# Two activation sums of the up projection: from GpSimd to VectorE, and later in the order

## The chip, the core and the metric

The kernel runs on one core of one Trainium2 chip. A core has TensorE (PE in the profile) for matrix products, VectorE (DVE), ScalarE (ACT), GpSimd (POOL) and SyncE (SP). SP and POOL also issue transfers here: SP's go through queue q1 of the profile, POOL's through q0. The metric is the device time of one execution in microseconds. The time before is the median of three runs; a profiled execution has a time of its own, and a span (first to last instruction) a little shorter than that.

## The reference, cut to what matters

One layer of an encoder on 512 rows of width 1024: a mixing part (a recurrent group and an attention group), then a feed-forward part, which the change lies in.

```python
x = x + concat(RMSNorm(rnn_out), RMSNorm(attn_out)) @ W_out
x = x + relu(RMSNorm(x) @ W_up)^2 @ W_down      # W_up 1024 x 4096, W_down 4096 x 1024
```

All of it is float32.

## The kernel before

**Products.** A float32 product is made of three reduced-precision ones (`mm3`, lines 319 to 322): both operands are split into a high part (ScalarE copies to fp32r: `whi`, `hh`) and a remainder (VectorE subtracts: `wlo`, `hl`), and high x high, high x low, low x high are summed in PSUM.

**Fewer products.** The up and down projections use a scheme with seven products of 2 x 2 blocks in place of eight. It needs sums of weight blocks and sums of activation blocks. The weight sums are mostly made by transfers that POOL issues and that add to what lies in SBUF (`accum_op=OP.add`); the activation sums are made by the engines in `h_sum` (line 1328). With `a = hm[k]` and `b = hm[k+4]` (the normalised, transposed activations), each 128 x 512, `left` and `right` the halves of the sequence, there are four sums:

- t1 = b.right - a.right, by VectorE
- t2 = -a.left - t1, by VectorE
- t3 = a.left - a.right, by GpSimd
- 22 = a.left - b.left + t1, by GpSimd in two instructions

Each sum has four quarters (k = 0 to 3) of 128 x 256; two quarters make one tile `hsum`. After every second quarter SP stores the tile to DRAM (`hsd`, line 1343, 256 KB), from where the second half of the projection loads it again. Two tiles make a sum, and `split_h` splits each of them (ScalarE `hh` line 1359, VectorE `hl` line 1362).

**Steps.** The up projection runs in two halves (`half` 0 and 1) of 28 steps each. A step is named by block column and product, for example 8:21, and has 24 products of 128 x 256 (lines 1547 to 1553). The first half goes 0:11, 8:11, 4:11, 0:21, 8:21, 4:21, 0:t1, 8:t1, 0:t2, 0:22, 0:t3, 8:t2, 8:22, 4:t1, 0:t4, 8:t3, 4:t2, 8:t4 and on. While step s computes, the weights of step s + 3 are split (`feed`, line 307: `whi` at product pair 2, `wlo` at pair 4). The dictionary `late` hangs further work on a step and a pair n.

**Order.** PE, ACT, DVE and POOL execute in the order in which the program is written. SP's order is made by a planner before the ninth step and is the written one from there on. What is late on an in-order engine delays all behind it.

**Buffers.** A plain weight block goes into one of three `wraw` buffers; `emit_dma` (line 225) loads the next one when `wlo` of an earlier block is made (line 270). Blocks that need sums lie in one of four `tw` buffers: `load_t` (line 1187) loads them on SP, `add_t` (line 1194) and `conv_lo` (lines 278 and 286) add further blocks through POOL, and line 282 adds a block with VectorE. The tiles of 128 x 512 share 45 slots.

**Around the beginning.** The product with W_out ends with the steps "s1" and "22" of `OSEQ`. VectorE adds its results into `x1n` (line 1218), PE transposes these (`h2_t`, line 1221), ScalarE writes `h2h` (line 1229) and `hm` (line 1231), and VectorE the remainder `h2l` (line 1234). The second half of the transposes stands inside steps 0:11 and 8:11.

Of the kernel before, what the change touches and what calls it, by code (L numbers as in the profile page):

```python
# [15 lines left out]
OP = mybir.AluOpType  # L16
# [85 lines left out]
def hybrid_kernel(ctx: ExitStack, tc, xw0, xw, xn, w_in, w_v, w_out, w_up, w_dn, gates, vecs, bias, fg, out):  # L102
    nc = tc.nc
# [9 lines left out]
    stt = nc.vector.scalar_tensor_tensor  # L113
    NG = 45

    def g_(name, dt=FT, shape=(P, S)):
        return work.tile(list(shape), dt, name=name, tag="g", bufs=NG)
# [633 lines left out]
    for n, (k, tt) in enumerate(steps):  # L751
        c = C_V + k // 2
# [434 lines left out]
    def load_t(half, n, f0, adds=True):  # L1187
        t = work.tile([P, 1024], FT, name="tw", tag="tw", bufs=4)
        nc.sync.dma_start(t, ublock(half, "12", f0))
        raws[cq[half, f0, n]] = t  # L1190
        if adds:
            add_t(half, n, f0)

    def add_t(half, n, f0):
        for b in {"t1": ("11",), "t2": ("11", "22"), "t3": ("22",) if (half, f0) in ADDED else ()}[n]:
            nc.gpsimd.dma_start(raws[cq[half, f0, n]], ublock(half, b, f0), accum_op=OP.add)
# [24 lines left out]
    def h2_t(k, tag):  # L1221
        if not hb:
            hb["h"] = big.tile([P, KD, S], FR, name="h2h", tag="bigB")
            hb["l"] = [t[:, j, :] for c in ("bigC", "bigD") for t in (big.tile([P, KD // 2, S], FR, name="h2l", tag=c),) for j in range(KD // 2)]
        pt = ps_("pxt", tag)
        n, j = k // 4, k % 4
        for tt in range(4):
            nc.tensor.transpose(pt[:, tt * P:(tt + 1) * P], x1n[tt, n][:, j * P:(j + 1) * P], ident)
        act(hb["h"][:, k, :], pt, AF.Copy, scale=vec("mg", k))
        hm[k] = g_("hm")  # L1230
        act(hm[k], pt, AF.Copy, scale=vec("mg", k))

    def h2_l(k):
        nc.vector.tensor_tensor(hb["l"][k], hm[k], f(hb["h"])[:, k, :], op=OP.subtract)
# [29 lines left out]
    for w in OSEQ:  # L1264
        for i in range(4):
            tt, k = i // 2, i % 2
# [59 lines left out]
    left, right = slice(0, TH), slice(TH, S)  # L1326

    def h_sum(n, k):
        m, c = k // 2, slice((k % 2) * TH, (k % 2 + 1) * TH)
        if k % 2 == 0:  # L1330
            hsum[n, m] = hsr[n, m] = g_("hsum")
        a, b, o = hm[k], hm.get(k + 4), hsr[n, m][:, c]
        if n == "t1":
            nc.vector.tensor_tensor(o, b[:, right], a[:, right], op=OP.subtract)
        elif n == "t2":
            stt(o, a[:, left], -1.0, hsr["t1", m][:, c], op0=OP.mult, op1=OP.subtract)
        elif n == "t3":
            nc.gpsimd.tensor_tensor(o, a[:, left], a[:, right], op=OP.subtract)
        else:
            nc.gpsimd.tensor_tensor(o, a[:, left], b[:, left], op=OP.subtract)  # L1340
            nc.gpsimd.tensor_tensor(o, o, hsr["t1", m][:, c], op=OP.add)
        if k % 2:
            nc.sync.dma_start(hsd[SUMS.index(n)][:, m * S:(m + 1) * S], hsr[n, m])

    hsr = {}
# [11 lines left out]
    def h_hi(n, m):  # L1357
        hsp[n, m] = (g_("hh", FR), g_("hl", FR))
        act(hsp[n, m][0], hsum[n, m], AF.Copy)

    def h_lo(n, m):
        nc.vector.tensor_tensor(hsp[n, m][1], hsum.pop((n, m)), f(hsp[n, m][0]), op=OP.subtract)
# [139 lines left out]
    def add_s1(half, ts, q):  # L1502
        t = raws[cd_[half] + 2 * q + 1] = ts[:, q, :]
        nc.gpsimd.dma_start(t, wblock(half, "12", q), accum_op=OP.add)
# [9 lines left out]
    for half in range(2):  # L1514
# [58 lines left out]
        def split_h(n, m):  # L1573
            def run():
                h_hi(n, m)
                h_lo(n, m)
            return run

        def xt(tt, n):
            return lambda: x1_sq(tt, n)  # L1580
# [16 lines left out]
        if half == 0:  # L1597
            def more():
                t, r = raws[cq[0, 12, "t3"]], st.pop("r")
                nc.vector.tensor_tensor(t, t, r, op=OP.add)  # L1600

            def sums(*a):
                return lambda: [h_sum(n, k) for n, k in a]

            def turn(js):
                def run():
                    for j in js:
                        h2_t(j, "et" if j < 6 else "pj")
                        h2_l(j)
                return run  # L1610

            late.update({(0, "11", 0): lambda: conv_lo(C_WA + 8), (0, "11", 3): lambda: conv_lo(C_WA + 9), (0, "11", 6): turn((4, 5)), (8, "11", 1): turn((6, 7)),
                         (0, "11", 1): sums(*[("t3", k) for k in range(4)]), (8, "11", 0): sums(("t1", 0), ("t1", 1)), (8, "11", 5): split_h("t1", 0),
                         (4, "11", 0): sums(("t1", 2), ("t1", 3), ("22", 0), ("22", 1), ("22", 2), ("22", 3)),
                         (4, "11", 1): split_h("t1", 1), (0, "21", 0): sums(("t2", 0), ("t2", 1)),
                         (0, "21", 5): split_h("t2", 0), (8, "21", 0): sums(("t2", 2), ("t2", 3)), (8, "21", 5): split_h("t2", 1),
                         (4, "21", 5): split_h("22", 0), (0, "t1", 5): split_h("22", 1),
                         (0, "t3", 3): put, (8, "t2", 3): put, (8, "t1", 1): split_h("t3", 0), (0, "t2", 1): split_h("t3", 1),
                         (8, "21", 2): lambda: load_t(0, "t1", 4, False), (4, "21", 2): lambda: add_t(0, "t1", 4), (8, "11", 7): lambda: add_t(0, "t3", 0),
                         (8, "t1", 5): lambda: load_t(0, "t3", 8),  # L1620
                         (8, "t2", 6): lambda: load_t(0, "t3", 4), (0, "t4", 3): put, (8, "t3", 0): lambda: load_t(0, "t1", 12, False), (4, "t2", 2): lambda: add_t(0, "t1", 12),
                         (4, "t3", 0): lambda: load_t(0, "t3", 12, False), (12, "t1", 7): more,
                         (0, "22", 7): xt(0, 0), (8, "t2", 7): xt(0, 1), (0, "t4", 7): room,
                         (12, "11", 5): lambda: add_s1(half, ts, 0), (4, "t4", 1): lambda: add_s1(half, ts, 1), (12, "t2", 1): lambda: add_s1(half, ts, 2), (12, "22", 5): lambda: add_s1(half, ts, 3)})
        else:
            late.update({(0, "11", 1): split_h(*HSEQ[6]), (0, "t1", 1): split_h(*HSEQ[7])})
# [100 lines left out]
        if half == 1:  # L1727
            b = 6 * NQ
# [89 lines left out]
```

## Time and profile before

| | |
|---|---|
| time, median of 3 runs | 528.49 us (526.54 to 528.83) |
| time of the profiled execution | 526.84 us |
| its span | 525.1 us |
| PE busy | 515.9 us (98%) |
| DVE busy | 428.3 us (82%) |
| ACT busy | 361.4 us (69%) |
| POOL busy | 85.2 us (16%) |
| DMA, mean over the span | 208 GB/s |
| granted TensorE clock | 0.998 |

A row of a timeline reads: start in us, duration in us, engine, line, operation, output<-input, shape, count, and in brackets the idle time before it with what ended it. A row of waits reads: who waited for whom, us in total, times, the longest. A row of windows gives the window, its length, the busy time of each engine with its number of instructions in brackets, the granted clock, the busy share of the DMA engines and GB/s. A line on a queue gives packets, MB and share of the time of 16 DMA engines.

### The profile page before, as it was taken

Reading aid. Unit: us, or ns where it says so; the run is one execution under the profiler, and the core shown is the slowest. Engines: PE = TensorE matmul, PEld = TensorE weight load, DVE = VectorE, ACT = ScalarE, POOL = GpSimd, SP = SyncE. Lnnn points to the kernel's source line nnn. Section 1 sums busy time; section 2 is a strip of 40 time slices with the busy share of each in tenths; the row PEclk is TensorE's granted clock in tenths of the full one; section 3 lists DMA queues with packets and bytes.
Section 4 is the critical chain, followed back from the end, with each engine's and each line's share of the span. In section 5 each row is a group of like instructions: output and inputs, shape, how many; then the busy total and the mean of one; then the engine's idle time right before and its main releaser. Section 6 shows DMA issues by size and latency. Waiting matters only on the chain.

```text
span 525.1 us, 8396 instructions
## 1 busy us (share of the span) xinstructions
PE 515.9 (98%) x3093; PEld 445.7 (85%) x3093; DVE 428.3 (82%) x655; ACT 361.4 (69%) x581; POOL 85.2 (16%) x109
## 2 busy tenths in 40 slices
PE   9999999999999998999999999999999999999995
PEld 7857888778787788999999888888999999888884
DVE  6998995887877889778689986889665977987885
ACT  7579946668765847577868965566567677655664
POOL 0182000000000427420112131001101300131000
PEclk9999999999999999999999999999999999999999
DMA  8736545358796499698879999986987497699704
GB/s 287 227 94 196 162 144 180 111 161 223 189 291 214 91 192 254 231 250 217 240 160 309 272 267 273 303 301 161 281 266 175 110 226 209 161 299 259 180 2 160
DMA packets 41465, 109.34 MB, mean 208 GB/s; under 512 B 5168, under 2 KB 13488, under 8 KB 41424
## 3 DMA queue, kind: packets, MB, share of 16 engines
q1 hardware_dynamic: 32576, 78.63, 44.7%
q0 software_dynamic: 8704, 29.99, 30.6%
q8 instruction: 24, 0.39, 0.3%
q10 hardware_dynamic: 144, 0.20, 0.1%
q14 instruction: 17, 0.14, 0.1%
HBM read 99.78 MB, written 4.29 MB: 198 GB/s over the span
## 4 chain that ended last, share of the span: by engine, by line
PE 85%; DMA 5%; DVE 4%; issue 3%; ACT 1%; POOL 1%; DVEq 0%; POOLq 0%; ACTq 0%
PE pd L320 10%; PE pd L321 10%; PE pd L322 10%; PE pu L320 7%; PE pu L321 7%; PE pu L322 7%; DMA tw<-in_w_up_dram 4%; PE pqk L320 3%; PE pqk L322 3%; PE pqk L321 3%; PE pt L850 2%; PE ps L814 2%; PE pwo L320 2%; PE pwo L322 2%; PE pwo L321 2%
## 5 line engine op out<-in xcount | busy, mean ns | idle before, releaser
L270 DVE TENSOR_TENSOR wlo<-wraw,whi 128x1024 fp32r<-128x1024 f32 x70 | 86.3, 1236 | 27.3 <-ACT whi L248 27.2
L248 ACT ACTIVATE whi<-wraw 128x1024 fp32r<-128x1024 f32 x66 | 69.3, 1053 | 38.4 <-PE pd L322 15.3
L321 PE MATMUL pd<-wlo,ah 128*128 128x512 f32 (+1 forms) x195 | 75.2, 386 | 0.0
L320 PE MATMUL pd<-whi,ah 128*128 128x512 f32 (+1 forms) x195 | 75.2, 386 | 0.0
L322 PE MATMUL pd<-whi,al 128*128 128x512 f32 (+1 forms) x195 | 75.2, 386 | 0.0
L320 PE MATMUL pu<-hh,whi 128*128 128x256 f32 x256 | 72.4, 283 | 0.0
L321 PE MATMUL pu<-hl,whi 128*128 128x256 f32 x256 | 72.4, 283 | 0.0
L322 PE MATMUL pu<-hh,wlo 128*128 128x256 f32 x256 | 72.4, 283 | 0.0
L270 DVE TENSOR_TENSOR wlo<-tw,whi 128x1024 fp32r<-128x1024 f32 x41 | 50.0, 1220 | 18.6 <-ACT whi L248 18.6
L248 ACT ACTIVATE whi<-tw 128x1024 fp32r<-128x1024 f32 x42 | 44.3, 1056 | 25.2 <-DMA tw<-in_w_up_dram 12.0
L322 PE MATMUL pu<-h2h,wlo 128*128 128x256 f32 x184 | 52.2, 283 | 0.9 <-DVE wlo L270 0.9
L320 PE MATMUL pu<-h2h,whi 128*128 128x256 f32 x184 | 52.3, 284 | 0.1
L321 PE MATMUL pu<-h2l,whi 128*128 128x256 f32 x184 | 52.0, 283 | 0.0
L320 PEld LDWEIGHTS pu<-hh,whi 128*128 128x128 f32 x256 | 49.2, 192 | 0.0
L321 PEld LDWEIGHTS pu<-hl,whi 128*128 128x128 f32 x256 | 49.2, 192 | 0.0
L322 PEld LDWEIGHTS pu<-hh,wlo 128*128 128x128 f32 x256 | 49.2, 192 | 0.0
L322 PEld LDWEIGHTS pd<-whi,al 128*128 128x128 f32 x195 | 36.6, 188 | 7.4
L320 PEld LDWEIGHTS pd<-whi,ah 128*128 128x128 f32 x195 | 36.6, 188 | 7.3
L321 PEld LDWEIGHTS pd<-wlo,ah 128*128 128x128 f32 x195 | 36.6, 188 | 7.3
L248 ACT ACTIVATE whi<-ts 128x1024 fp32r<-128x1024 f32 x24 | 25.4, 1059 | 21.4 <-PE pd L322 14.7
L270 DVE TENSOR_TENSOR wlo<-ts,whi 128x1024 fp32r<-128x1024 f32 x24 | 29.3, 1222 | 8.9 <-ACT whi L248 8.6
L322 PEld LDWEIGHTS pu<-h2h,wlo 128*128 128x128 f32 x184 | 35.3, 192 | 1.1 <-DVE wlo L270 1.1
(282 smaller groups left out, 1251.4 us busy)
## 6 DMA issues: line engine op xcount, KB each, us to landing
wraw<-in_w_up_dram SPq DMA_DIRECT2D x24, 512.0 KB, 4.3
wraw<-in_w_dn_dram SPq DMA_DIRECT2D x24, 512.0 KB, 9.9
ts<-in_w_dn_dram POOLq DMA_DIRECT2D x24, 512.0 KB, 12.0
tw<-in_w_up_dram POOLq DMA_DIRECT2D x22, 512.0 KB, 7.9
tw<-in_w_up_dram SPq DMA_DIRECT2D x17, 512.0 KB, 6.1
wraw<-in_w_in_dram SPq DMA_DIRECT2D x13, 512.0 KB, 4.2
ts<-in_w_dn_dram SPq DMA_DIRECT2D x8, 512.0 KB, 6.5
tw<-in_w_dn_dram SPq DMA_DIRECT2D x8, 512.0 KB, 6.8
```

Source lines behind the costliest of these rows:

```text
L248: act(hi, raws[i], AF.Copy)
L270: nc.vector.tensor_tensor(lo, r, f(splits[i][0]), op=OP.subtract)
L320: nc.tensor.matmul(o, lhsT=a[0], rhs=b[0], start=bool(first), stop=False, skip_group_check=on)
L321: nc.tensor.matmul(o, lhsT=a[0], rhs=b[1], start=False, stop=False, skip_group_check=on)
L322: nc.tensor.matmul(o, lhsT=a[1], rhs=b[0], start=False, stop=bool(last), skip_group_check=on)
L814: nc.tensor.matmul(psq[p, u][e][:, :NK], lhsT=qs_[p, a][r, P * qt:P * qt + P], rhs=kks[p][r, b, w:w + NK], start=i == 0, stop=i == 2)
L850: nc.tensor.transpose(pt[:, i * P:(i + 1) * P], en[h][qt][:, k:k + P], ident)
```

## The change

VectorE makes t3 and 22. The sum 22 is one instruction for a quarter instead of two: -b.left - t2, which is the same as a.left - b.left + t1. Both stand later: t3 moves from step 0:11 to 8:t1, and 22 from 4:11 to 0:t1; the splits of 22 go from 4:21 and 0:t1 to 0:t1 and 8:t1, those of t3 from 8:t1 and 0:t2 to 0:t2 alone (pairs 1 and 5). The stores to `hsd` follow the sums. GpSimd only issues transfers in this part.

```diff
         elif n == "t3":
-            nc.gpsimd.tensor_tensor(o, a[:, left], a[:, right], op=OP.subtract)
+            nc.vector.tensor_tensor(o, a[:, left], a[:, right], op=OP.subtract)
         else:
-            nc.gpsimd.tensor_tensor(o, a[:, left], b[:, left], op=OP.subtract)
-            nc.gpsimd.tensor_tensor(o, o, hsr["t1", m][:, c], op=OP.add)
+            stt(o, b[:, left], -1.0, hsr["t2", m][:, c], op0=OP.mult, op1=OP.subtract)
...
-                         (0, "11", 1): sums(*[("t3", k) for k in range(4)]), (8, "11", 0): sums(("t1", 0), ("t1", 1)), (8, "11", 5): split_h("t1", 0),
-                         (4, "11", 0): sums(("t1", 2), ("t1", 3), ("22", 0), ("22", 1), ("22", 2), ("22", 3)),
+                         (8, "11", 0): sums(("t1", 0), ("t1", 1)), (8, "11", 5): split_h("t1", 0),
+                         (4, "11", 0): sums(("t1", 2), ("t1", 3)),
...
-                         (4, "21", 5): split_h("22", 0), (0, "t1", 5): split_h("22", 1),
-                         (0, "t3", 3): put, (8, "t2", 3): put, (8, "t1", 1): split_h("t3", 0), (0, "t2", 1): split_h("t3", 1),
+                         (0, "t1", 0): sums(*[("22", k) for k in range(4)]), (0, "t1", 5): split_h("22", 0), (8, "t1", 1): split_h("22", 1),
+                         (0, "t3", 3): put, (8, "t2", 3): put, (8, "t1", 3): sums(*[("t3", k) for k in range(4)]), (0, "t2", 1): split_h("t3", 0), (0, "t2", 5): split_h("t3", 1),
```

## The prediction

> **What bounds the kernel now.** The page first: its opening lines say that PE is busy for all but 2% of the span. So a change in another engine can only pay where PE waits, and the next view is the waits of PE over the whole span.
>
> ```profile
> span 525.1 us, 8396 instructions
> PE 515.9 (98%) x3093; PEld 445.7 (85%) x3093; DVE 428.3 (82%) x655; ACT 361.4 (69%) x581; POOL 85.2 (16%) x109
> ```
> ```profile
> PE pxt L1228 <- DVE x1n L1218: 1.4, 1, 1.4
> PE pu L322 <- DVE wlo L270: 0.9, 1, 0.9
> ```
>
> Two waits of any size, both for VectorE, and both by the sixth step of the up projection. PE's timeline has them exactly, with a small third one:
>
> ```profile
> 201.89 0.27 PE L1228 MATMUL pxt<-ident,x1n 128*128 128x128 f32 x1
> 203.61 0.99 PE L1228 MATMUL pxt<-ident,x1n 128*128 128x128 f32 x7 [1.44 <-DVE x1n L1218]
> ...
> 218.01 0.28 PE L320 MATMUL pu<-h2h,whi 128*128 128x256 f32 x1
> 218.13 0.28 PE L321 MATMUL pu<-h2l,whi 128*128 128x256 f32 x1
> 219.33 0.39 PE L322 MATMUL pu<-h2h,wlo 128*128 128x256 f32 x1 [0.92 <-DVE wlo L270]
> ...
> 222.07 0.28 PE L320 MATMUL pu<-hh,whi 128*128 128x256 f32 x1
> ...
> 253.63 0.28 PE L322 MATMUL pu<-hh,wlo 128*128 128x256 f32 x1
> 254.01 0.39 PE L320 MATMUL pu<-h2h,whi 128*128 128x256 f32 x1
> ```
>
> A product of this stage starts 0.12 us after the one before (218.01, 218.13), so a step of 24 takes 2.88. The gaps above that pace: 203.61 - 201.89 - 0.12 = 1.60, 219.33 - 218.13 - 0.12 = 1.08, and 254.01 - 253.63 - 0.12 = 0.26. Together 2.94 us, the most that this stage can give. Now VectorE and GpSimd before the first gap:
>
> ```profile
> 197.44 3.59 DVE L1234 TENSOR_TENSOR h2l<-hm,h2h 128x512 fp32r<-128x512 f32 x2
> ...
> 201.61 1.28 DVE L1234 TENSOR_TENSOR h2l<-hm,h2h 128x512 fp32r<-128x512 f32 x2
> 202.81 0.74 DVE L1218 SCALAR_TENSOR_TENSOR x1n<-pwo,nrc,x 128x512 f32<-128x512 f32 x1
> 203.47 3.48 DVE L270 TENSOR_TENSOR wlo<-wraw,whi 128x1024 fp32r<-128x1024 f32 x3
> ```
> ```profile
> 198.03 3.60 POOL L1338 TENSOR_TENSOR hsum<-hm 128x256 f32<-128x256 f32 x4
> ```
>
> The same pair of `h2l` takes 3.59 us where GpSimd makes t3 beside it and 1.28 where it doesn't: 2.31 lost. The last `x1n`, which PE waits for, is late by it. Before the second gap the pattern repeats with sum 22:
>
> ```profile
> 212.71 1.75 DVE L270 TENSOR_TENSOR wlo<-wraw,whi 128x1024 fp32r<-128x1024 f32 x1 [2.13 <-ACT whi L248]
> 214.39 0.68 DVE L1362 TENSOR_TENSOR hl<-hsum,hh 128x512 fp32r<-128x512 f32 x1
> 216.44 1.16 DVE L1362 TENSOR_TENSOR hl<-hsum,hh 128x512 fp32r<-128x512 f32 x1 [0.70 <-ACT hh L1359]
> 217.52 1.75 DVE L270 TENSOR_TENSOR wlo<-wraw,whi 128x1024 fp32r<-128x1024 f32 x1
> 219.20 0.74 DVE L1336 SCALAR_TENSOR_TENSOR hsum<-hm,hsum 128x256 f32<-128x256 f32 x2
> 219.87 1.21 DVE L270 TENSOR_TENSOR wlo<-tw,whi 128x1024 fp32r<-128x1024 f32 x1
> ```
> ```profile
> 216.30 0.74 POOL L1340 TENSOR_TENSOR hsum<-hm 128x256 f32<-128x256 f32 x1
> 217.12 1.07 POOL L1341 TENSOR_TENSOR hsum<-hsum 128x256 f32<-128x256 f32 x1
> ```
>
> `wlo` takes 1.75 twice here and 1.21 alone (219.87), `hl` 1.16 beside GpSimd (216.30) and 0.68 alone: 0.54, 0.54 and 0.48 lost. The `wlo` that starts at 217.52 is the one PE waits for in step 4:21.
>
> **The change, part by part.** First, what goes: twelve GpSimd instructions. Their own time is on no path to PE; their cost is what they hold up.
>
> *First gap.* Without t3 the first `h2l` pair takes 1.28. The later order is then held by ScalarE, which writes the last needed `hm` here:
>
> ```profile
> 199.62 0.68 ACT L1231 ACTIVATE hm<-pxt,vt 128x512 f32<-128x512 f32 x1
> 211.61 1.06 ACT L248 ACTIVATE whi<-wraw 128x1024 fp32r<-128x1024 f32 x1 [2.19 <-DMA wraw<-in_w_up_dram]
> ```
>
> It ends at 200.30; one `h2l` (half of 1.28) and one `x1n` (0.74) later it is 201.7, against 203.55 before. PE wants it at 201.89 + 0.12 = 202.01. So the whole gap goes, 1.60 us, with 0.3 to spare.
>
> *Second gap.* It is a chain: VectorE's `wlo` (203.47) frees `wraw`, SP loads the weights of 8:21, ScalarE waits for them (211.61) and VectorE for ScalarE (212.71). With VectorE 1.9 earlier, the load is too.
>
> ```profile
> 204.75 2.55 SPq L229 DMA_DIRECT2D wraw<-in_w_up_dram  x3
> ```
>
> The stores of t3 also leave SP's queue ahead of it. `wlo` of 8:21 then starts at or before 212.71 - 1.9 = 210.8 and takes 1.21; 0.54 + 0.48 + 0.54 of blocking go behind it. The `wlo` of 4:21, which ended at 217.52 + 1.75 = 219.27, ends 1.9 + 0.54 + 0.48 + 0.54 = 3.5 earlier at 215.8 (with ScalarE's `hh` and `whi` in between it may be 216.2). PE, itself 1.60 earlier, wants it at 218.25 - 1.60 = 216.65. The second gap goes too: 1.08. What is late next is nothing I find before step 0:t1.
>
> *The sums on VectorE.* A pair of quarters by the same form of instruction takes 0.74 (219.20), so eight take at most 2.96, in steps 0:t1 and 8:t1. The cover is VectorE's lead:
>
> ```profile
> 228.09 1.21 DVE L270 TENSOR_TENSOR wlo<-tw,whi 128x1024 fp32r<-128x1024 f32 x1
> 229.23 0.68 DVE L1362 TENSOR_TENSOR hl<-hsum,hh 128x512 fp32r<-128x512 f32 x1
> 237.89 1.23 DVE L282 TENSOR_TENSOR tw<-tw,wraw 128x1024 f32<-128x1024 f32 x1 [3.54 <-DMA tw<-in_w_up_dram]
> 240.23 1.22 DVE L270 TENSOR_TENSOR wlo<-tw,whi 128x1024 fp32r<-128x1024 f32 x1
> ```
>
> The last `hl` of t3 was done at 229.91. With 3.5 of lead and 2.96 of sums it is 229.4; step 0:t3 begins at 222.07 + 4 x 2.88 = 233.59, in the new time 2.68 earlier, 230.9. Margin 1.5, so the sums cost nothing. Without the lead they would end at 232.9 and PE would stand for 2.0.
>
> *The stores.* Four stores of 256 KB move from about 200 and 216 to between 220 and 227, into a window where the DMA engines are full:
>
> ```profile
> 213.00:216.00 3.00, 3.00 (x28) 3.00 (x27) 2.74 (x4) 0.91 (x3) 0.84 (x2) 1.00 0.22 47
> ...
> 228.00:231.00 3.00, 3.00 (x27) 3.00 (x27) 1.91 (x3) 1.52 (x3) 0.48 (x1) 1.00 1.04 261
> ```
> ```profile
> q1 hardware_dynamic: 32576, 78.63, 44.7%
> q0 software_dynamic: 8704, 29.99, 30.6%
> ```
> ```profile
> 229.33 0.33 SPq L1189 DMA_DIRECT2D tw<-in_w_up_dram  x1
> ```
>
> A megabyte on q1 takes 0.447 x 525.1 / 78.63 = 2.99 us of all engines, so four stores of 0.262 MB take 3.1. Behind them on SP stands the load of 229.33 (weights of 8:t3), for which VectorE sits idle 3.54 until 237.89, and after that comes the `wlo` of 4:t1, done at 240.23 + 1.22 = 241.45. PE's step 4:t1 begins at 222.07 + 7 x 2.88 = 242.23 and wants it two products later, at 242.47: 1.0 of slack. With PE 2.68 earlier the load must land at least 1.7 earlier than 237.89. For it: nearly all transfers of this window are issued 3.5 earlier, and the window 213 to 216, in which the DMA engines were 78% idle (2.3 us) because `wraw` was not free, fills. Against it: 3.1 of stores. By these the landing is between 3.5 - 3.1 = 0.4 and 0.4 + 2.3 = 2.7 earlier, or 3.5 if the stores overtake nothing. I take 2.4, nearer to the upper end since the idle window is the direct result of the stall that goes, so no stall; 0.4 would cost 1.3.
>
> [...]
>
> *Sum.* 1.60 + 1.08 + 0 + 0 = 2.68; the third gap (0.26) probably goes too, as PE there waits for a VectorE chain that begins with the same load, so 2.8. On the profiled execution's 526.84 that is 524.0. That execution lies 1.65 under the median of the runs: 526.54 and 526.84 stand beside 528.49 and 528.83, mean 527.7. A median of new runs may fall into either group, so I state 527.7 - 2.8 = 524.9.
>
> **The rivals.** *Part given back.* The load of 8:t3 lands only 0.4 earlier, and PE stands 1.3 in step 4:t1. Gain 1.5 (0.9 to 2.3): 525.3 in the profiled terms, 526.2 as stated. For it: the DMA share of 1.04. Against it: the idle 2.3 us.
>
> *Slower: the stores delay the load.* VectorE's lead is eaten by the sums, the load goes out at 229.33 as before, and the four stores lie ahead of it in SP's queue. The queues share the engines about evenly here:
>
> ```profile
> q1 hardware_dynamic: 1571, 4.42, 48.9%
> q0 software_dynamic: 576, 2.10, 42.0%
> ```
>
> (window 215 to 242.) At the full rate it lands 3.1 later, at half rate 6.2. It decides from 1.0 of delay; then the loss is 3.1 - 1.0 = 2.1 to 6.2 - 1.0 = 5.2, whatever was gained earlier: 528.9 to 532.0 in the profiled terms, 529.8 to 532.9 as stated. Against it: the lead, and that the two stores of 22 are issued a step ahead of those of t3. [...]
>
> *VectorE becomes the bound.* The lead is not there and the sums hold up t3: PE loses 2.0 at 0:t3 but keeps 1.60 and perhaps 1.08. Gain about 0 to 0.7: 527.4 as stated. The margin of 1.5 is against it.
>
> **How the numbers follow.** Forecast 0.60, part given back 0.15, VectorE the bound 0.05, slower by the stores 0.20. A measurement of this kernel tells about 0.5% from no change, 2.64 us. The forecast's own range is a gain of 2.3 to 3.0, and 0.47 of its 0.60 lie over 2.64; the rest of it (0.13), the two middle cases (0.20) and 0.05 of the slow case are within; 0.15 are slower by more. The range reaches from the faster group less the whole 2.94 (526.54 - 2.94 = 523.6, down to 523.3 for the scatter) to the slower group less the smallest gain of the second case (528.49 - 0.9 = 527.6), and so leaves the slow case out.
>
> **What would show it.** In the changed profile: `h2l` pairs of 1.28 everywhere, `wlo` at 1.21; no wait of PE on `x1n` or on `wlo` at 4:21; `wlo` of 4:21 done by 216.2; the load of 8:t3 landing before 236.2. Wrong it would be by a new wait of PE between 0:t1 and 8:t4, above all at 4:t1, or by a first gap that is still there, which would mean that GpSimd wasn't what held the `h2l` pair.

## The result and the profile after

The changed kernel takes 530.80 us (median of 6 runs, 530.02 to 531.72), the kernel before 527.79 (6 runs, 526.54 to 528.83): a ratio of 1.0059 with a 95% interval of 1.0039 to 1.0078. It is slower, by 3.0 us. The profiled execution took 530.84 us, 4.0 more than that of before. The page of the changed kernel:

```profile
span 529.1 us, 8386 instructions
PE 518.2 (98%) x3093; PEld 447.8 (85%) x3093; DVE 426.5 (81%) x663; ACT 361.5 (68%) x581; POOL 71.7 (14%) x97
```

GpSimd has 13.5 us and 12 instructions less, VectorE 8 more instructions and yet 1.8 us less. The edit does what it says. PE has 2.3 us more of busy time for the same 3093 products, the first strange thing. The waits of PE (who for whom, total, times, longest):

```profile
PE pu L320 <- DVE a L1387: 2.9, 2, 2.4
PE pu L322 <- DVE wlo L270: 1.2, 1, 1.2
```

Both rows of before are gone. In their place PE waits for `a` (line 1387, the addition in `quad_evac` that empties a PSUM bank; 1388 before) and for a `wlo`. Its timeline has the two long ones in step 4:t1, and the short one later, at the start of 4:t4:

```profile
240.24 0.28 PE L322 MATMUL pu<-hh,wlo 128*128 128x256 f32 x1
242.88 0.35 PE L320 MATMUL pu<-hh,whi 128*128 128x256 f32 x1 [2.36 <-DVE a L1387]
243.08 0.28 PE L321 MATMUL pu<-hl,whi 128*128 128x256 f32 x1
244.53 0.38 PE L322 MATMUL pu<-hh,wlo 128*128 128x256 f32 x1 [1.17 <-DVE wlo L270]
...
248.74 0.29 PE L320 MATMUL pu<-h2h,whi 128*128 128x256 f32 x1
...
271.68 0.28 PE L322 MATMUL pu<-hh,wlo 128*128 128x256 f32 x1
272.53 0.36 PE L320 MATMUL pu<-h2h,whi 128*128 128x256 f32 x1 [0.57 <-DVE a L1387]
```

Above the pace of 0.12 these are waits of 242.88 - 240.24 - 0.12 = 2.52, 244.53 - 243.08 - 0.12 = 1.33 and 272.53 - 271.68 - 0.12 = 0.73. From 244.53 to 248.74 PE makes 22 products, which at 0.12 are 2.64 us; it takes 4.21. The windows show why (and, above them, the stage in which DMA engines were idle before):

```profile
210.00:213.00 3.00, 3.00 (x27) 3.00 (x26) 1.91 (x3) 2.06 (x3) 0.00 (x0) 1.00 0.65 251
213.00:216.00 3.00, 3.00 (x27) 3.00 (x26) 2.05 (x4) 2.38 (x4) 0.00 (x0) 1.00 0.78 264
216.00:219.00 3.00, 3.00 (x27) 3.00 (x26) 3.00 (x6) 2.21 (x3) 0.00 (x0) 1.00 0.47 119
...
243.00:246.00 3.00, 1.83 (x12) 1.63 (x13) 3.00 (x5) 2.97 (x6) 0.85 (x1) 0.89 0.52 175
246.00:249.00 3.00, 3.00 (x16) 3.00 (x16) 2.93 (x7) 2.94 (x6) 0.00 (x0) 0.54 0.96 153
```

The granted clock (the last but two of the numbers) falls behind the wait: 0.89 and 0.54, so (0.11 + 0.46) x 3 = 1.7 us of PE's work are lost there. VectorE and SP, from the start of the stage to the landing of the load of 8:t3:

```profile
198.42 1.28 DVE L1234 TENSOR_TENSOR h2l<-hm,h2h 128x512 fp32r<-128x512 f32 x2
...
201.92 0.74 DVE L1218 SCALAR_TENSOR_TENSOR x1n<-pwo,nrc,x 128x512 f32<-128x512 f32 x1
...
222.33 1.43 DVE L1340 SCALAR_TENSOR_TENSOR hsum<-hm,hsum 128x256 f32<-128x256 f32 x4
...
226.01 1.42 DVE L1338 TENSOR_TENSOR hsum<-hm 128x256 f32<-128x256 f32 x4
227.35 1.22 DVE L270 TENSOR_TENSOR wlo<-tw,whi 128x1024 fp32r<-128x1024 f32 x1
...
240.92 1.23 DVE L282 TENSOR_TENSOR tw<-tw,wraw 128x1024 f32<-128x1024 f32 x1 [8.52 <-DMA tw<-in_w_up_dram]
242.06 1.28 DVE L1387 TENSOR_TENSOR a<-v,pu 128x512 f32<-128x512 f32 x2
243.25 1.22 DVE L270 TENSOR_TENSOR wlo<-tw,whi 128x1024 fp32r<-128x1024 f32 x1
...
255.02 1.22 DVE L282 TENSOR_TENSOR tw<-tw,wraw 128x1024 f32<-128x1024 f32 x1
256.15 0.68 DVE L1387 TENSOR_TENSOR a<-v,pu 128x512 f32<-128x512 f32 x1
```
```profile
225.31 0.53 SPq L229 DMA_DIRECT2D wraw<-in_w_up_dram  x1
226.79 1.41 SPq L1342 DMA_DIRECT2D hsd<-hsum  x2
228.60 0.76 SPq L1189 DMA_DIRECT2D tw<-in_w_up_dram  x1
```

The `h2l` pair is back at 1.28. The eight sums take 1.43 + 1.42 = 2.85. The load of 8:t3 goes out at 228.60, right behind the two stores of t3 and right after the `wlo` that frees its buffer (227.35 + 1.22 = 228.57). VectorE then stands 8.52 us until it lands at 240.92, and behind the waiting line 282 stand the two `a` and the `wlo` that PE waits for.

This trace starts the stage later than that of before (the first `h2l` row at 198.42 against 197.44, both ahead of anything the change touches). From that row on, the load lands 240.92 - 198.42 = 42.50 us later here and 237.89 - 197.44 = 40.45 before: 2.05 later. Its way from issue to use was 237.89 - 229.33 = 8.56 before and is 240.92 - 228.60 = 12.32.

### The profile page after: what moved, and what is told of

It is laid out like the page before. It is cut to its first block, busy times and chain, and to the rows that moved or that the text cites. A ratio compares the mean times of both kernels' runs of the same rounds, so it can differ in the third digit from the quotient of the medians.

```text
span 529.1 us, 8386 instructions
## 1 busy us (share of the span) xinstructions
PE 518.2 (98%) x3093; PEld 447.8 (85%) x3093; DVE 426.5 (81%) x663; ACT 361.5 (68%) x581; POOL 71.7 (14%) x97
## 4 chain that ended last, share of the span: by engine, by line
PE 85%; DMA 6%; DVE 5%; issue 2%; ACT 1%; POOL 0%; DVEq 0%; ACTq 0%; SPq 0%
PE pd L321 10%; PE pd L320 10%; PE pd L322 10%; PE pu L320 6%; PE pu L321 6%; PE pu L322 6%; DMA tw<-in_w_up_dram 5%; PE pqk L320 3%; PE pqk L322 3%; PE pqk L321 3%; PE pwo L320 3%; PE pwo L322 3%; PE pwo L321 3%; PE pav L950 2%; PE pt L850 2%; PE ps L814 2%
## 5 line engine op out<-in xcount | busy, mean ns | idle before, releaser
L270 DVE TENSOR_TENSOR wlo<-wraw,whi 128x1024 fp32r<-128x1024 f32 x70 | 85.2, 1220 | 25.0 <-ACT whi L248 24.8
L320 PEld LDWEIGHTS pu<-h2h,whi 128*128 128x128 f32 x184 | 35.4, 192 | 0.8 <-ACT whi L248 0.7
## 6 DMA issues: line engine op xcount, KB each, us to landing
ts<-in_w_dn_dram POOLq DMA_DIRECT2D x24, 512.0 KB, 12.3
```

Of the source, the lines that this page charges most:

```text
L270: nc.vector.tensor_tensor(lo, r, f(splits[i][0]), op=OP.subtract)
L320: nc.tensor.matmul(o, lhsT=a[0], rhs=b[0], start=bool(first), stop=False, skip_group_check=on)
```

## The experiments

Five theories are told apart. **S**: the four stores that now stand ahead of the load of 8:t3 in SP's queue delay it. **G**: the adding transfers that GpSimd issues crowd it out, stores or not. **V**: the sums on VectorE take up its lead and send the load out late. **W**: a second limit, the chain behind 8:t3, keeps PE from gaining much whatever happens at 4:t1. **C**: the wait makes PE's clock fall, which costs something on top. "Behind" a load means later in SP's written order. The line numbers of the variants lie a few off those of the changed kernel. The kernels that move stores use

```python
if k % 2 and n in ("t1", "t2"):        # 22 and t3: stored by h_stores
    h_store(n, m)
```

and place `h_stores(...)` in `late`.

**The changed kernel, all four stores behind the load.** `(8, "t3", 1): h_stores("22", "t3")`

> The changed kernel, with the four stores of t3 and 22 issued behind the weight loads of step 8:t3 (some 20 us later); sums and splits stay as changed. Theory S (the four stores lie ahead of the load of the weights of 8:t3 in SP's queue, so VectorE's add at L282 and the wlo behind it come late and PE stands at 4:t1): the load lands 3 us earlier or more, no wait of PE over 0.3 us at 4:t1, and the gaps at the transposes and at 4:21 stay away, so ratio to before 0.993 to 0.997 (about 525). Rival G (GpSimd, free of sums, issues its adding transfers earlier and closer together and these crowd out the load) and rival V (the sums on VectorE send the load out late): the wait at 4:t1 stays, 2 us or more, ratio 1.003 to 1.007.

527.75 us against 527.66; ratio 1.0006 (0.9990 to 1.0023). The load and its use:

```profile
228.09 0.33 SPq L1189 DMA_DIRECT2D tw<-in_w_up_dram  x1
```
```profile
236.64 1.22 DVE L282 TENSOR_TENSOR tw<-tw,wraw 128x1024 f32<-128x1024 f32 x1 [4.51 <-DMA tw<-in_w_up_dram]
```

It takes 8.55 us where it took 12.32, with the same sums and the same transfers of GpSimd. The wait at 4:t1 shrinks from 3.85 to 0.37. S holds, and G as a cause by itself falls. But the gain expected (0.993 to 0.997) is not there, since a new wait of 1.98 stands at 4:t4: the stores, issued at 244.54, now lie ahead of later weights.

**The kernel before, with the stores alone moved.** The sums stay on GpSimd; VectorE rewrites one column of each tile (128 x 1) where the change would make it, so that the store cannot go earlier.

> The kernel before, with the sums on GpSimd where they were, and only the four stores of t3 and 22 moved to the place that they have in the changed kernel; to hold them there VectorE rewrites one column of each tile first (four instructions of 128x1, about 0.15 us each). S: the gaps of 1.6 and 1.1 us at the transposes and at 4:21 stay, the load for 8:t3 lands 2 to 6 us later and PE waits 1 to 5 us more at 4:t1: ratio 1.003 to 1.012. G and V: no new wait over 0.5 us, ratio 0.998 to 1.002.

533.50 us; ratio 1.0118 (1.0099 to 1.0137), double the loss of the whole change.

```profile
230.31 0.85 SPq L1189 DMA_DIRECT2D tw<-in_w_up_dram  x1
```
```profile
245.12 1.23 DVE L282 TENSOR_TENSOR tw<-tw,wraw 128x1024 f32<-128x1024 f32 x1 [9.88 <-DMA tw<-in_w_up_dram]
```

14.81 us from issue to use: the stores alone do it, with neither the sums nor the lead.

**No stores of t3 and 22 at all.** The second half loads t1's tiles in their place, so that part of the output is computed from other sums.

> The changed kernel without the four stores of t3 and 22: the second half loads t1's tiles in their place, so it computes with other sums there. S + W: the load for 8:t3 lands where it did with the stores moved late (236.6, 1.2 us earlier than in the kernel before), no wait over 0.4 us at 4:t1, and behind it only the 1.2 us that the chain of transfers has gained is kept at 4:t4: ratio 0.996 to 0.999. S alone: all 2.7 us of the two first gaps are kept, 0.994 to 0.996.

526.98 us; ratio 0.9977 (0.9954 to 1.0000). The load takes 8.4 us, 4:t1 has no wait. PE waits 252.69 - 251.54 - 0.12 = 1.03 us at 8:t4 instead:

```profile
251.54 0.28 PE L322 MATMUL pu<-hh,wlo 128*128 128x256 f32 x1
252.69 0.39 PE L320 MATMUL pu<-h2h,whi 128*128 128x256 f32 x1 [0.86 <-DVE a L1387]
```

Without any store the change gains 0.2% (0.5% at the most by the interval), and part of what was gained earlier comes back as a wait: W.

**All four stores eight steps later still**, behind the last load of that stage: `(12, "t2", 0): h_stores("22", "t3")`

> The changed kernel, with all four stores of t3 and 22 in step 12:t2 (about 273 us), behind the transfers of the second limit too. S + W: as without the stores, since in the weight loads behind them there are over 2 us of slack: 0.996 to 0.999; better than with the stores at step 8:t3 (1.0006) by 0.5 to 2 us. S alone: 0.994 to 0.996.

527.09 us; ratio 0.9984 (0.9968 to 1.0000). The wait at 4:t4 is 0.20 in place of 1.98, so the stores further back no longer cost anything there. That the time is better than in the first run is not shown, since the two intervals overlap. In this profile the load of 8:t3 goes out 1.3 us later than in the first run (31.65 and 30.39 from the `h2l` row), though the order up to it is the same.

**One pair ahead, the other late.** First, 22's stores stay in their place and t3's go to (8, "t3", 1):

> The changed kernel, with only t3's two stores behind the weight loads of 8:t3; those of 22 stay. S: half the load ahead of it, so the load lands 1 to 2 us earlier than in the changed kernel, and the wait at 4:t1 falls from 3.9 us to between 0 and 2: ratio 0.996 to 1.002. G and V: as the changed kernel, 1.003 to 1.007.

530.02 us; ratio 1.0053 (1.0034 to 1.0073), worse than expected. The load is no longer late (8.2 us); the largest loss is at 4:t4, 1.92 us of wait for weights behind the moved stores, and there the clock falls:

```profile
270.00:273.00 3.00, 2.91 (x18) 2.94 (x19) 3.00 (x4) 0.15 (x1) 0.85 (x1) 0.73 0.11 16
273.00:276.00 3.00, 3.00 (x21) 3.00 (x20) 2.00 (x3) 2.97 (x6) 0.00 (x0) 0.71 1.02 165
```

Then with the late pair at (12, "t2", 0), once t3's and once 22's:

> Dose. Of the changed kernel's four stores, 22's two stay where the change puts them, ahead of the load of 8:t3; t3's two go to (12, t2, 0), behind all four loads. S (stores ahead of the load delay it, each by its share): between no store ahead (0.998) and four (1.006), so 1.000 to 1.004; the load's tile lands 1 to 2.5 us later than with none, and 4:t1 waits 0.3 to 2 us. G and V (adding transfers, or the sums on VectorE, delay it and the stores do not): as the changed kernel, 1.004 to 1.008, with 2 us or more of wait at 4:t1.

> Dose, the other half. t3's two stores stay where the change puts them, ahead of the load of 8:t3, and 22's two go to (12, t2, 0). S: 1.000 to 1.004, as in the run that keeps 22's, since both have two stores of the same size ahead; if one is clearly slower than the other, the place counts beside the number. G and V: 1.004 to 1.008, with 2 us or more of wait at 4:t1.

With 22's pair ahead 527.14 us, ratio 0.9969 (0.9946 to 0.9991), better than expected; with t3's pair ahead 531.02, ratio 1.0042 (1.0017 to 1.0067). The second lies just above what S gives and within what G and V give (1.004 to 1.008), with 2.88 us of wait at 4:t1 (2.14 in the first); but the sums and GpSimd's transfers are the same in both runs, so the place of the stores makes the difference. Two stores of the same size, and only one place hurts: t3's pair goes out 1.8 us ahead of the load (225.82 and 227.62), 22's pair 4 us ahead of it or more (by 224.86; the load at 228.85). The loads took 10.7 and 11.3 us. Here the profiles are poor witnesses: that with 22's pair took 528.23, over its median, and that with t3's pair 527.99, the fastest of ten with a median of 531.02.

**t3 early on VectorE, with its stores.** `(8, "11", 2): sums(t3)` in place of `(8, "t1", 3)`.

> The changed kernel, with t3's sums on VectorE in step 8:11, pair 2, so that its two stores go out at about 211 us; its splits stay where the change puts them. S: as with the two stores behind the load, or better, since these stores fall into a stretch in which the DMA engines have room: wait at 4:t1 between 0 and 2 us, ratio 0.995 to 1.001. V: half of the added VectorE work is off the way to the load, so the wait falls by about 0.7 us to 3.2: ratio 1.002 to 1.006. G: as the changed kernel.

527.08 us; ratio 0.9989 (0.9974 to 1.0004). The load goes out at 226.76 but takes 12.5 us behind 22's stores, and 3.19 us of wait are left at 4:t1 where S expected 0 to 2; that profile is of the slowest of the ten runs (529.17).

**The same, with 22's stores at (12, "t2", 0).**

> The changed kernel, with t3's sums and stores in step 8:11 (pair 2) and 22's two stores only in step 12:t2 (about 273 us); the sums of 22 stay where the change puts them. Theory S + W: the four stores no longer lie ahead of the load for 8:t3, and VectorE has four sums less ahead of that load, so it goes out about 1.3 us earlier than with only the stores moved and lands at about 235; the next limit is W, the adding transfer for the weights of 12:t1, whose high part ScalarE makes at 258.7 in the kernel before: PE at 4:t4 has almost no slack against it, so PE keeps only what that transfer gains, 1.5 to 2.7 us. Ratio to before 0.995 to 0.998. S alone (no second limit): 0.994 to 0.996. G (crowding by GpSimd's transfers): 1.003 to 1.007.

526.06 us against 527.88; ratio 0.9975 (0.9957 to 0.9992): faster than the kernel before, as the run with 22's pair ahead was. Its profile has one wait left in this stage, 0.56 at 8:t4.

```profile
226.82 0.33 SPq L1189 DMA_DIRECT2D tw<-in_w_up_dram  x1
```
```profile
236.28 1.23 DVE L282 TENSOR_TENSOR tw<-tw,wraw 128x1024 f32<-128x1024 f32 x1 [4.14 <-DMA tw<-in_w_up_dram]
```

**t3's sums and stores behind the load**, at (8, "t1", 6):

> The changed kernel, with t3's four sums three pairs later in step 8:t1, behind the wlo of 0:t3 that frees the buffer for the load of 8:t3; its two stores then stand behind that load in SP's queue, 22's two ahead of it. S + W: load issued 1.3 us earlier than in the changed kernel and two stores less ahead of it, so it lands 2 to 4 us earlier; the wait at 4:t1 falls from 3.9 to between 0 and 2: ratio 0.996 to 1.001. V alone (the sums hold the load, the stores don't matter): 1.3 us of the 3.9 go, 1.003 to 1.005. G: as the changed kernel.

527.55 us; ratio 0.9999 (0.9986 to 1.0013). Out at 226.87, landed at 239.78, 12.9 us. t3's sums no longer stand ahead of the `wlo` that frees the buffer, so the load leaves 1.3 us earlier than in the changed kernel (28.90 and 30.18 from the `h2l` row), and t3's stores are behind it: V is part of it. But the load lands only 0.7 earlier (2 to 4 expected) and 3.14 of wait are left at 4:t1: an early issue did not bring an early landing while 22's stores were ahead.

**The clock.** The changed kernel with 8 extra products ahead of 4:t1, zero weights into a sum that is still open:

> The changed kernel with 8 extra products on PE ahead of the first product of 4:t1 (zero weights, added to a sum that is still open, so that nothing changes in the result). They stand in the wait of 2.5 us and should take 1.7 to 2 us of it. C (the wait lets PE's clock fall, and the slow stretch behind it costs 1.65 us on top): no window with a granted clock near 0.5 behind 4:t1, and 1.001 to 1.004 in place of 1.006. Rival (the loss is the wait alone, the clock falls whatever stands in it, or the extra products cost as much as they save): clock near 0.5 as before, or 1.005 to 1.008. Both: the load of 8:t3 lands as late as in the changed kernel, 12 us or more after its issue.

534.27 us; ratio 1.0127 (1.0106 to 1.0148). It missed its aim: the extra products wrote to a bank that ScalarE had yet to read, and waited themselves.

```profile
245.63 0.58 PE L1544 MATMUL pu<-ident,const-float32-0.0 128*128 128x128 f32 x1 [5.25 <-ACT v L1378]
```

The same into the bank of block column 4, which nothing is waiting to read:

> As the run before (8 extra products on PE ahead of 4:t1, zero weights), but added to the open sum of block column 4, whose last reader is done since about 222 us. In the run before they were added to that of block column 8 and so waited themselves, 5.25 us, for ScalarE's copy of it. Now they should start at once and take 1.7 us of the 2.5 us of wait. C (the wait lets PE's clock fall, which costs 1.65 us on top): no granted clock near 0.5 behind 4:t1, and 1.001 to 1.004. Rival (the fall of the clock does not come from the wait, or costs nothing on top): clock near 0.5 as before, or 1.005 to 1.008 without it.

530.92 us; ratio 1.0062 (1.0041 to 1.0084), no change. The extra products ran at once, but 1.37 and 1.33 of wait were left, and the clock fell all the same (0.81 from 243 to 246, 0.62 from 246 to 249). So both waits were filled, 12 products ahead of 4:t1 and 6 behind its second one, with the changed kernel run beside it:

> As the run before, but with 12 extra products ahead of 4:t1 (16 passes took 1.71 us, so 24 take 2.6) and 6 more between the second and the third product of 4:t1 (1.3 us), so that both waits are filled and under 0.5 us of each is left. C (the wait lets the clock fall, 1.65 us on top): no granted clock near 0.5 behind 4:t1 in the profile, mean clock of the runs 0.996 or more, and 1.000 to 1.004, at least 1 us under the changed kernel of the same call. Rival (the loss is the wait alone): the time of the changed kernel, within 0.7 us.

> The changed kernel itself, beside the run above: 1.004 to 1.008, with mean clocks of 0.991 to 0.995.

530.39 us (529.34 to 532.03, 10 runs), ratio 1.0050 (1.0029 to 1.0071), against 531.78 (530.37 to 532.97, 6 runs), ratio 1.0075 (1.0049 to 1.0101). The windows behind 4:t1, first with both waits filled, then the changed kernel again:

```profile
243.00:246.00 3.00, 3.00 (x26) 2.98 (x27) 3.00 (x5) 2.97 (x6) 0.85 (x1) 1.00 0.57 175
246.00:249.00 3.00, 3.00 (x28) 3.00 (x27) 2.93 (x7) 2.94 (x6) 0.00 (x0) 1.00 0.87 141
```
```profile
243.00:246.00 3.00, 1.55 (x7) 1.38 (x8) 3.00 (x6) 2.80 (x6) 0.84 (x1) 0.81 0.54 175
246.00:249.00 3.00, 3.00 (x19) 3.00 (x19) 2.93 (x7) 2.97 (x5) 0.01 (x1) 0.62 0.71 106
```

With PE kept at work the clock stays at 1.00, though the load lands as late (240.94 and 241.31); the mean clock of the runs is 0.996 to 0.999 against 0.990 to 0.996. So the wait does make it fall. The medians differ by 1.4 us, more than the rival allows (0.7), but the runs overlap, and the time stays above the range that C expected: by the medians 2.3 of the 3.7 us lost (530.39 and 531.78 against 528.05) are not the clock's. PE, on time again, stands 0.95 us at 8:t4:

```profile
242.91 0.36 PE L1557 MATMUL pu<-hh,whi 128*128 128x256 f32 x1 [0.67 <-DVE a L1388]
...
256.88 0.38 PE L321 MATMUL pu<-h2h,whi 128*128 128x256 f32 x1 [0.79 <-DVE a L1388]
```

## Where the time is decided

That last wait is the key, and rows of before had it. Between the two rows of line 282 lie 255.02 - 240.92 = 14.10 us after the change, and 252.14 - 237.89 = 14.25 before. Over the other profiles it is 13.9 to 14.3, but 14.53 with the stores alone, and 16.51 in the first run with extra products, where PE itself came 5.4 us late. After the landing VectorE and ScalarE work through a fixed order, ScalarE with hardly a gap (0.27 us from 242.77 on, after the change), and the `a` that PE needs for 8:t4 stands right behind the second line 282. In the kernel before, PE starts 8:t4 at 254.01, 16.12 after the landing; with 22's stores ahead at 255.50, 15.95 after 239.55; in the filled kernel at 256.88, 15.94 after 240.94. In all nine profiles in which the clock did not fall at 4:t1 it is 15.8 to 16.1, each time after a wait of 0.26 to 1.07 at the start of 8:t4. In these the landing sets when 8:t4 begins, whatever PE gained or lost ahead of it. Where the clock fell, PE comes to 8:t4 without a wait, and a little later: 16.4 to 16.5 after the landing in five profiles, 17.4 with the stores alone and 19.4 in the first run with extra products.

The table tests this. Reference is the start of the first `h2l` row in each trace (197.44 before); landing is the first row of line 282 less that, and rest is the span less that. Both as differences to before (40.45 and 327.66).

| profile | landing | rest | |
|---|---|---|---|
| t3 early, 22's stores late | -2.22 | -2.71 | |
| no stores | -1.97 | -1.96 | |
| all stores at 12:t2 | +0.31 | +0.27 | |
| 22's ahead | +0.34 | +0.08 | |
| t3's ahead | +1.07 | +1.18 | clock fell |
| t3's sums behind | +1.36 | +1.17 | |
| t3 early, 22's ahead | +1.38 | +2.31 | clock fell |
| changed kernel | +2.05 | +3.02 | clock fell |
| changed kernel again | +3.06 | +3.14 | clock fell |
| both waits filled | +3.04 | +2.69 | |
| stores alone | +7.32 | +8.29 | clock fell |
| 8 extra products, column 4's bank | +2.81 | +3.26 | clock fell |
| 8 extra products, bank still to be read | +2.61 | +5.67 | 5.42 of wait at 4:t1, clock fell |
| all stores at 8:t3 | -1.51 | +0.14 | 1.98 of wait at 4:t4 |
| 22's ahead, t3's at 8:t3 | -0.58 | +2.61 | 1.92 at 4:t4, clock fell there |

Where nothing else stands in the way, the rest follows the landing within 0.5 us. Where the clock fell at 4:t1, and PE did not wait for its own extra products, up to 1 us comes on top and not 1.7, because PE would otherwise stand about 1 us at 8:t4 anyway. Not all of that is the clock's: the profile of the changed kernel has 0.73 of wait at 4:t4 and that with t3 early and 22's ahead 0.77, which the repeat of the changed kernel has not. Of the 3.02 of the changed kernel 2.05 are the landing, 16.48 - 16.12 = 0.36 lie between the landing and 8:t4, and 0.61 come behind it. The last two rows lose theirs behind 8:t4, by stores that were moved to a bad place.

Each row is one execution, so the table shows what goes with what and does not rank the kernels; the medians above do that. With 22's pair ahead, for one, the median is 0.3% under that of before although the load of its profile lands 0.34 later.

## Why the prediction was wrong, point by point

The forecast was 524.9; the rival *slower: the stores delay the load* is what happened, inside its 529.8 to 532.9. In part that is luck: it let the load go out as late as before and gave PE 1.0 of slack, and neither was so.

*First gap: right.* The `h2l` pair takes 1.28, PE does not wait for `x1n`. GpSimd was what held it: in the kernel before, one `h2l` alone takes 2.99 (from 198.03) beside four instructions of GpSimd that take 3.60 together (1.05 to 1.24 each), and 0.68 where none runs beside it. The 2.31 that it loses are more than any one of the four takes; by what means they hold it is not shown.

*Second gap: right.* No wait at 4:21; the `wlo` that PE waited for there is no longer late. In two later profiles (t3's stores at 8:t3, all stores at 12:t2) 0.45 and 0.42 are left, since the weights ahead of it came later: ScalarE waits 2.8 and 2.7 us for them, 1.3 in the changed kernel.

*The sums: right as priced, wrong in what they touch.* 2.85 us against 2.96, and PE waits for none of them. But they stand ahead of the `wlo` of 0:t3, which frees the buffer of the load of 8:t3. The prediction used the same lead twice: once to cover the sums, and again to issue "nearly all transfers of this window" 3.5 earlier. From the `h2l` row the load goes out at 228.60 - 198.42 = 30.18, against 229.33 - 197.44 = 31.89: 1.7 earlier.

*The stores: priced nearly right, and the terms set against them failed.* They were 3.1 us; the load took 12.32 in place of 8.56, 3.8 more. The first counterweight, an issue 3.5 earlier, was 1.7. The second, 2.3 us from idle DMA engines, was not there: from 210 to 219 they are idle for (0.35 + 0.22 + 0.53) x 3 = 3.3 us, and that is no use to a load whose buffer comes free at 228.57. So the landing is 3.8 - 1.7 = 2.1 later where 2.4 earlier was taken. This is the step that failed. In the four later profiles with the same order up to that load it is 2.6 to 3.1 later.

*The sum: right in size only if the landing had been.* It added up the two gaps that go. The prediction asked whether the load was early enough for 4:t1, with 1.0 of slack, and gave the third gap 0.26 as a bonus. That gap was the limit: in the kernel before PE had already caught up with the chain behind the landing, and time gained ahead of it turns into wait at 8:t4 (1.03 us without any stores). The gain is about the advance of the landing: without the stores 1.96 for 1.97, with t3 early and 22's stores late 2.71 for 2.22. A landing 2.4 earlier would so have given near the 2.8 of the forecast, and for another reason than the two gaps. The two kernels that are clear of the time before gain 0.25% and 0.31%, about half of the forecast; the profile with the 2.71 is of one of the faster runs (524.82, median 526.06).

*Not foreseen:* the fall of the clock (0.89 and 0.54 in two windows of 3 us, 1.7 us of PE's work).

Open is the way of the load itself. With 22's pair ahead it took 8.2, 10.7, 12.5 and 12.9 us in four profiles, of which the first two have the same order up to the load; a profile is a single execution, and the times of one kernel lie between 1.7 and 6 us apart. That t3's pair hurts more since it goes out 1.8 us ahead of the load, and 22's has drained by then, fits the medians of those two runs but is argued, not shown: with 22's pair ahead the load took 12.5 and 12.9 as well. How much of the loss in the medians is the clock's is open too.

## What to carry to other kernels

Work moved to a later place takes its transfers along: list what stands behind them in the queue, and whose buffer the engine's next instruction frees, before counting an engine's lead as cover, and count that lead once. Before summing the waits of a bottleneck engine, look for the smallest and last one: if it ends a chain that starts from a transfer, the earlier waits are worth only what that transfer gains (here 1.96 us for a landing 1.97 earlier, without the stores). A store that nobody reads soon belongs where no load that somebody waits for stands close behind it; moved behind the next load only, it stood ahead of the one after that here (1.98 us at 4:t4).

## What the runs showed of the hardware

PE's granted clock fell after waits shorter than its slow stretch: in one profile after 1.92 us (22's ahead, t3's at 8:t3: 0.73 and 0.71 in two windows of 3 us), in another after 1.37 + 1.33 with two products between (8 extra products, column 4's bank: 0.81 and 0.62), but not after 1.98 (all stores at 8:t3) nor after 1.82 + 1.32 (t3's sums behind), with 1.00 in all windows of 3 us around them. Why waits of so nearly the same length came out differently is not shown. In windows of 0.4 us the granted clock of the changed kernel is 1.00 up to 245.2, 0.68 in the next, 0.50 from 245.6 to 248.4 and 0.55 in the one after, and the slow stretch is about 3.4 us (1.7 us of work lost at 0.50). With t3's stores ahead the ten runs of one kernel divide by it: six with a mean clock of 0.990 or 0.991 took 530.86 to 532.71, four with 0.993 to 0.999 took 527.99 to 530.27. A later landing would bring both a longer wait and a fall of the clock, so this division does not price the clock.

Stores ahead of a load in SP's queue went with a longer way of the load, from issue to use. With none of these four stores ahead, or t3's far ahead of it, a load of 512 KB took 8.4 to 9.5 us in four profiles; with all four ahead 12.3 to 13.1 in the five profiles of the changed kernel and of those with extra products; with two issued 1.8 us ahead of it 11.3 in one profile, and with two issued earlier still (22's pair) 8.2 to 12.9 in four.
